# Low parts of k stored for both heads over all 128 partitions, in a block with stick-breaking attention

## The chip, the cores and the metric

The kernel runs on one core of a Trainium2 chip, as one launch. The metric is the device time in microseconds (us); the time before is the median of three runs. One further execution was taken with a profiler; all durations of single instructions come from it. The core has five engines that run their own instruction streams and wait for one another through semaphores: TensorE (PE in the profile, its weight loads PEld), VectorE (DVE), ScalarE (ACT), GpSimd (POOL) and SyncE (SP), which here only issues DMAs.

## The reference

A transformer block on 1024 positions of width 1024: attention over 8 heads of 64 beside a gated linear recurrence, then an MLP with squared ReLU. What the change concerns is the score product in the attention:

```python
def stick_breaking_attention(q, k, v):
    ...
    for blk in range(S // BLOCK_Q):
        q0 = blk * BLOCK_Q
        end = q0 + BLOCK_Q
        z = jnp.einsum('bqhd,bkhd->bhqk', qf[:, q0:end], kf[:, :end]) * scale
        ...
        mask = kpos < qpos
        log_one_minus = jnp.where(mask, jax.nn.log_sigmoid(-z), 0.0)
        suffix = lax.cumsum(log_one_minus, axis=3, reverse=True) - log_one_minus
        log_w = jax.nn.log_sigmoid(z) + suffix
        w = jnp.where(mask, jnp.exp(log_w), 0.0)
        outs.append(jnp.einsum('bhqk,bkhd->bqhd', w, vf[:, :end]))

def hybrid_mixer(h, w_in, ...):
    proj = h @ w_in
    q, k, v, xl, gl = jnp.split(proj, ...)
    q = rms_norm(q.reshape(B, S, N_ATTN_HEADS, HEAD_DIM), q_norm_g)
    k = rms_norm(k.reshape(B, S, N_ATTN_HEADS, HEAD_DIM), k_norm_g)
    ...
    attn = stick_breaking_attention(q, k, v).reshape(B, S, ATTN_WIDTH)
    xl = causal_depthwise_conv(xl, conv_w, conv_b)
    lru = rg_lru(xl, ...) * jax.nn.gelu(gl)
    return jnp.concatenate([attn, lru], axis=-1) @ w_out
```

## The kernel before

**Split operands.** Products that need more than one pass's precision are made of parts. A value is written as a high part in the format fp32r and a low part, the rest (`lo_part`, L59: a subtraction on an engine that is passed in). Most products add three matmuls (`mm3`, L70): low by high, high by low, high by high.

**Stages.** The input is normalised and transposed into `hTh` and `hTl` (high and low). For each of four pairs of heads `p`, `in_proj` (L193) projects 256 positions at a time (`tp` from 0 to 3) to q, k and v. The recurrence follows (`lru_tile`), then the attention of the four pairs mixed with the in-projection of the next pair and with the gates (`gate`, L479); then the out-projection (`po`) and the MLP in two groups (`up_group`, `down_group`). `ORDER` (L34) names the sequence in which the jobs of the attention stage are written: I is an in-projection, A an attention job (pair, head of the pair, block of 256 queries), G a gate, O and W loads of weights, Y a DMA that sums parts of the MLP's weights. The kernel is built by a scheduler, which sets the order on each engine from its own estimate of times; a changed instruction can therefore move others.

**In-projection.** After the norm, `qs` holds for each head its high part of q beside its low part, 64 columns each; `ks` holds the high part of k twice, and `kl` the low part of k once, for both heads of the pair side by side. Transposes on TensorE (matmuls with the identity `identr`) turn them into banks of PSUM: `pq`, `pk` with four each, `pl` with two. Copies bring the banks to `qT` and `kH` (2 x 256 columns) and `kL` (256 columns). All three banks are the one buffer of the pool `ps_t`, so they follow each other. In `qT[:, h]` 64 partitions hold the high part of q and the other 64 its low part; in `kH[:, h]` both halves hold the high part of k. In `kL`, 64 partitions belong to each head.

**Attention.** For a row block of 128 queries and up to 512 keys (`k0`), two matmuls make the scores `z`: L431 over all 128 partitions gives (high + low of q) by high of k, and L432 over the head's 64 partitions `hs` gives high of q by low of k. The block on the diagonal adds the mask by a third matmul (L434). Two sigmoids on ScalarE follow (L436, L437), a running product from the right on VectorE (L441) and a product on GpSimd (L442). The weights `w` are transposed (`pw`, L452), split (`wth`, `wtl`) and multiplied by v (`av`, L461); `ob` goes to the array `mix_d` in DRAM. There are 96 such score blocks.

**Gates.** `gate(c, ch)` loads two arrays (`gx` of `rs_d`, `hl` of `lru_d`), makes a projection `pgl` from `hTh` and `hTl`, and works on VectorE (L487, L489), ScalarE and GpSimd (L491, L492). Its tiles are buffers of the in-projection: `gx` has the tag `raw`, `hl` that of `ks` or `kl`. The loads of `x1` (L586), for the out-projection, go into the place of `hTh`, and so wait for the last gate's projection; on SP they stand in one queue with all other loads.

Of the kernel before, what the change touches and what calls it, by code (L numbers as in the profile page):

```python
# [10 lines left out]
F32R = mybir.dt.float32r  # L11
# [8 lines left out]
P = 128  # L20
S = 1024
D = 1024
NT = S // P
KC = D // P
HD = 64
# [18 lines left out]
def kernel(ctx, tc, x, norm1_g, w_in, conv_w, conv_b, w_rg, b_rg, w_ig, b_ig,  # L44
                             lam, q_norm_g, k_norm_g, w_out, norm2_g, w_up, w_down, out):
    nc = tc.nc
# [12 lines left out]
    def lo_part(eng, lo, src, hi):  # L59
        ins = eng.tensor_tensor(lo, src, hi.bitcast(F32), op=ALU.subtract)  # L60
        if eng is nc.gpsimd:
            mark(ins)
# [4 lines left out]
    def mark(ins):  # L67
        marked[:] = [ins.ins]
# [13 lines left out]
    ps_t = pool(ctx, "ps_t", bufs=1, space=PSUM)  # L82

    def bank(pl, shape, name):
        return pl.tile([P] + shape, F32, tag=pl.name, name=name)
# [33 lines left out]
    identr = const.tile([P, P], F32R, name="identr")  # L119
# [35 lines left out]
    mp = pool(left1, "misc")  # L155
# [32 lines left out]

    def in_proj_open(p, qp):
        return (qp.tile([P, 2, S], F32R, tag="qT", name=f"qT{p}"), qp.tile([P, 2, S], F32R, tag="kH", name=f"kH{p}"),  # L190
                qp.tile([P, S], F32R, tag="kL", name=f"kL{p}"), qp.tile([P, NT, 2, P], F32R, tag="vv", name=f"vv{p}"))

    def in_proj(p, qkv, ws, tp):  # L193
        qT, kH, kL, vv = qkv
        raw = mp.tile([P, 2, 4, HD], F32, tag="raw", name=f"raw{p}{tp}", bufs=2)
        for tt in range(2):
            t = 2 * tp + tt
            pd = bank(ps_d, [384], f"pd{p}{t}")
            for kc in range(KC):
                wh, wl = ws[kc]  # L200
                mm3(pd, hTh[:, kc, t * P:(t + 1) * P], hTl[:, kc, t * P:(t + 1) * P], wh, wl, kc == 0, kc == KC - 1)
            rs = rstd1[:, t:t + 1]
            nc.scalar.mul(raw[:, tt].rearrange("p a d -> p (a d)"), pd[:, 0:256], rs)
            pvv = pd[:, 256:384].rearrange("p (h d) -> p h d", h=2)
            nc.scalar.mul(vv[:, t, :, 0:HD], pvv, rs)
            nc.vector.scalar_tensor_tensor(vv[:, t, :, HD:P], pvv, rs, vv[:, t, :, 0:HD].bitcast(F32), op0=ALU.mult, op1=ALU.subtract)  # L206
        sq = mp.tile([P, 8, HD], F32, tag="sq", name=f"sq{p}{tp}")
        raw8 = raw.rearrange("p t a d -> p (t a) d")
        nc.vector.tensor_tensor(sq, raw8, raw8, op=ALU.mult)
        ssq = small.tile([P, 8], F32, tag="ssq8", name=f"ssq{p}{tp}")  # L210
        nc.vector.tensor_reduce(ssq, sq, axis=AX.X, op=ALU.add)
        rstd = rsqrt_mean(ssq, HD, 8)
        nc.vector.tensor_tensor(raw8, raw8, rstd.unsqueeze(2).broadcast_to([P, 8, HD]), op=ALU.mult)
        nc.gpsimd.tensor_tensor(raw[:, :, 0:2, :], raw[:, :, 0:2, :], qkg, op=ALU.mult)
        qs = mp.tile([P, 2, 2, 2, HD], F32R, tag="qs", name=f"qs{p}{tp}")
        ks = mp.tile([P, 4, 2, HD], F32R, tag="ks", name=f"ks{p}{tp}")
        kl = mp.tile([P, 2, 2, HD], F32R, tag="kl", name=f"kl{p}{tp}")
        for h in range(2):
            nc.scalar.copy(qs[:, :, h, h, :], raw[:, :, h, :])
            lo_part(nc.vector, qs[:, :, h, 1 - h, :], raw[:, :, h, :], qs[:, :, h, h, :])  # L220
        for tt in range(2):
            nc.scalar.copy(ks[:, 2 * tt:2 * tt + 2], raw[:, tt, 2:4, :].unsqueeze(2).broadcast_to([P, 2, 2, HD]))
            lo_part(nc.gpsimd, kl[:, tt], raw[:, tt, 2:4, :], ks[:, 2 * tt:2 * tt + 2, 0, :])
        cols = slice(256 * tp, 256 * tp + 256)
        pq = bank(ps_t, [2, 256], f"pq{p}{tp}")
        for h in range(2):
            for tt in range(2):
                nc.tensor.matmul(pq[:, h, tt * P:(tt + 1) * P], qs[:, tt, h].rearrange("p a d -> p (a d)"), identr, start=True, stop=True)
        nc.scalar.copy(qT[:, :, cols], pq)
        pk = bank(ps_t, [2, 256], f"pk{p}{tp}")  # L230
        for h in range(2):
            for tt in range(2):
                nc.tensor.matmul(pk[:, h, tt * P:(tt + 1) * P], ks[:, 2 * tt + h].rearrange("p a d -> p (a d)"), identr, start=True, stop=True)
        nc.vector.tensor_copy(kH[:, :, cols], pk)
        pl = bank(ps_t, [256], f"pl{p}{tp}")
        for tt in range(2):
            nc.tensor.matmul(pl[:, tt * P:(tt + 1) * P], kl[:, tt].rearrange("p a d -> p (a d)"), identr, start=True, stop=True)
        nc.vector.tensor_copy(kL[:, cols], pl)


    right1 = ExitStack()
# [97 lines left out]
    for tp in range(2, NT // 2):  # L339
# [4 lines left out]
        if tp == 3:  # L344
            scale_row(1)
        in_proj(0, qkv0, wpair, tp - 1)
    in_proj(0, qkv0, wpair, NT // 2 - 1)
    xstack.close()

# [64 lines left out]
    def attention(p, h, c, qkv):  # L414
        qT, kH, kL, vv = qkv
        hs = slice(HD * h, HD * h + HD)
        os = slice(HD - HD * h, P - HD * h)
        wrow = []
        for r in (2 * c, 2 * c + 1):
            n = (r + 1) * P  # L420
            wps = {}
            nxt = None
            qr = slice(r * P, (r + 1) * P)
            for k0 in range((n - 1) // 512 * 512, -1, -512):
                kn = min(n - k0, 512)
                diag = k0 + kn == n
                g = ap.tile([P, 516], F32, tag="g", name=f"g{p}{h}{r}{k0}", bufs=NG)
                w = ap.tile([P, 512], F32, tag="w", name=f"w{p}{h}{r}{k0}", bufs=NW)
                wps[k0 // 512] = w
                z = bank(ps_z, [512], f"z{p}{h}{r}{k0}")[:, :kn]  # L430
                nc.tensor.matmul(z, qT[:, h, qr], kH[:, h, k0:k0 + kn], start=True, stop=False)  # L431
                nc.tensor.matmul(z, qT[hs, h, qr], kL[hs, k0:k0 + kn], start=False, stop=not diag)  # L432
                if diag:
                    nc.tensor.matmul(z[:, kn - P:kn], identb, maskb, start=False, stop=True)  # L434
                    nc.gpsimd.memset(g[:, kn:kn + 1], 1.0)
                nc.scalar.activation(g[:, :kn], z, AF.Sigmoid, scale=-1.0)  # L436
                nc.scalar.activation(w[:, :kn], z, AF.Sigmoid)  # L437
                if not diag:
                    nc.vector.tensor_copy(g[:, kn:kn + 1], nxt)
                gr = g[:, :kn][:, ::-1]  # L440
                nc.vector.tensor_tensor_scan(gr, gr, gr, g[:, kn:kn + 1], op0=ALU.mult, op1=ALU.bypass)  # L441
                mark(nc.gpsimd.tensor_tensor(w[:, :kn], w[:, :kn], g[:, 1:kn + 1], op=ALU.mult))  # L442
                nxt = g[:, 0:1]
            wrow.append(wps)
        av = bank(ps_a, [256], f"av{p}{h}{c}")
        for m in range(c + 1):
# [11 lines left out]
            for jj in range(2):  # L458
                q0 = P if jj == 1 and m == c else 0
                for wt in (wtl, wth):  # L460
                    nc.tensor.matmul(av[:, q0:256], vv[:, 2 * m + jj, h, :], wt[:, 256 * jj:256 * jj + 256 - q0],  # L461
                                     start=m == 0 and jj == 0 and wt is wtl,
                                     stop=m == c and jj == 1 and wt is wth)
# [411 lines left out]
```

## Time and profile before

| what | time, us |
|---|---|
| median of the runs (1215.03 to 1216.63) | 1215.21 |
| the profiled execution | 1218.14 |
| its span, first to last instruction | 1216.4 |
| ahead of the first score product | 137 |
| score products, 96 blocks | 137 to 450 |
| from 540 to the end (rest of the out-projection, MLP) | 676 |

The profiled execution is 2.9 us above the median. In the profile a group's line gives source line, engine, operation and tiles (result <- operands), then the count, the busy time, the mean length of one and what the engine waited for ahead of it. "issue" is time in which an engine waited for nothing that the profile shows. A timeline gives the start and the length; matmuls overlap, so the time that one takes in a stream is read from start to start. 64*128 in a matmul's row means 64 rows of the array by 128 columns.

### The profile page before, as it was taken

How to read it: one execution, taken by the hardware profiler on the slowest of the kernel's cores; microseconds unless marked ns; L12 is line 12 of the kernel's file. 1: busy time of each engine (PE TensorE's matmuls, PEld its weight loads, DVE VectorE, ACT ScalarE, POOL GpSimd, SP SyncE). 2: the span in 40 equal slices, each digit the busy share in tenths (PEclk: the TensorE clock that was granted, in tenths of full speed). 3: DMA queues.
4: the chain of work that ended last, by engine and by line, in shares of the span. 5: the costliest groups of instructions: out<-in, count | busy, mean ns of one | idle time of the engine just before them, and what ended most of it. 6: DMA issues, size and time to landing. Idle time of an engine off the chain costs nothing.

```text
span 1216.4 us, 15273 instructions
## 1 busy us (share of the span) xinstructions
PE 1150.6 (95%) x5410; PEld 948.0 (78%) x5410; DVE 897.3 (74%) x1182; ACT 568.5 (47%) x991; POOL 586.5 (48%) x472
## 2 busy tenths in 40 slices
PE   7998899999999988998999989889999999999998
PEld 7976777789987766886888767678887887878887
DVE  6889997999898788226387769685843876699663
ACT  7554475665665564144433554233334335733331
POOL 1356764574355566102645746533317368483240
PEclk9999999799999978998999989989999999999999
DMA  8110026824505275200453788944412345442531
GB/s 262 48 49 35 18 96 130 227 66 145 122 5 112 89 256 181 101 1 35 141 188 130 201 241 287 224 142 139 141 35 87 122 144 191 158 148 73 193 132 69
DMA packets 91659, 157.05 MB, mean 129 GB/s; under 512 B 8848, under 2 KB 27328, under 8 KB 91584
## 3 DMA queue, kind: packets, MB, share of 16 engines
q1 hardware_dynamic: 79040, 122.54, 30.5%
q0 software_dynamic: 12544, 33.56, 11.8%
q8 instruction: 42, 0.69, 0.2%
q14 instruction: 33, 0.27, 0.1%
HBM read 145.58 MB, written 44.04 MB: 156 GB/s over the span
## 4 chain that ended last, share of the span: by engine, by line
PE 69%; DVE 13%; issue 8%; DMA 3%; POOL 3%; ACT 3%; SPq 0%; DVEq 0%; ACTq 0%; POOLq 0%
PE p L633 22%; PE pa L633 11%; PE pb L633 5%; PE pc L633 4%; PE pd L71 3%; PE pd L72 3%; PE pd L73 3%; PE po L71 3%; PE po L72 2%; PE po L73 2%; PE av L461 2%; PE z L432 2%; PE pw L452 2%; DVE g L441 2%; DVE sl_u L60 2%
## 5 line engine op out<-in xcount | busy, mean ns | idle before, releaser
L442 POOL TENSOR_TENSOR w<-w,g 128x128 f32<-128x128 f32 (+3 forms) x96 | 99.7, 1044 | 107.7 <-DVE g L441 52.7
L60 DVE TENSOR_TENSOR ml_p<-rp,mh_p 128x1024 fp32r<-128x1024 f32 x56 | 110.3, 1971 | 28.1 <-ACT mh_p L544 28.1
L441 DVE TENSOR_TENSOR_SCAN g<-g 128x128 f32<-128x128 f32 (+3 forms) x96 | 112.6, 1185 | 8.0 <-ACT g L436 5.4
L544 ACT CAST sh_p<-U 128x1024 fp32r<-128x1024 f32 x48 | 50.5, 1051 | 131.0 <-PE pa L633 59.2
L633 PE MATMUL pa<-mh_p,sl_p 128*128 128x512 f32 x256 | 100.7, 393 | 7.1 <-DVE sl_p L60 6.8
L767 POOL TENSOR_TENSOR rp<-rp,qp 128x1024 f32<-128x1024 f32 x24 | 69.0, 2876 | 70.3 <-DMA qp<-in_w_down_dram 39.8
L633 PE MATMUL pa<-ml_p,sh_p 128*128 128x512 f32 x256 | 100.3, 392 | 0.0
L633 PE MATMUL pa<-mh_p,sh_p 128*128 128x512 f32 x256 | 100.1, 391 | 0.0
L71 PE MATMUL pd<-wh_p,hTl 128*128 128x384 f32 x256 | 90.9, 356 | 7.3 <-DVE vv L206 5.0
L72 PE MATMUL pd<-wl_p,hTh 128*128 128x384 f32 x256 | 89.8, 351 | 0.1
L73 PE MATMUL pd<-wh_p,hTh 128*128 128x384 f32 x256 | 88.3, 345 | 0.0
L60 DVE TENSOR_TENSOR sl_p<-U,sh_p 128x1024 fp32r<-128x1024 f32 x38 | 63.4, 1668 | 30.7 <-ACT sh_p L544 30.7
L737 POOL TENSOR_TENSOR ru<-ru,rv 128x1024 f32<-128x1024 f32 x16 | 43.8, 2769 | 58.9 <-DMA rv<-sum_u 58.8
L544 ACT CAST mh_p<-rp 128x1024 fp32r<-128x1024 f32 x56 | 58.7, 1048 | 21.3 <-POOL rp L767 14.6
L633 PEld LDWEIGHTS pa<-mh_p,sl_p 128*128 128x128 f32 x256 | 48.5, 189 | 18.2 <-DVE sl_p L60 7.5
L662 POOL TENSOR_TENSOR U<-U 128x512 f32<-128x512 f32 x32 | 47.0, 1501 | 32.0 <-ACT U L660 32.0
L456 ACT CAST wth<-pw 128x512 fp32r<-128x512 f32 (+1 forms) x80 | 42.4, 545 | 38.0 <-PE pw L452 24.8
L436 ACT ACTIVATE g<-z 128x384 f32<-128x384 f32 (+3 forms) x96 | 47.8, 497 | 22.9 <-PE z L434 10.4
L71 PEld LDWEIGHTS pd<-wh_p,hTl 128*128 128x128 f32 x256 | 49.4, 193 | 11.0 <-DVE vv L206 6.7
L660 ACT ACTIVATE U<-U 128x512 f32<-128x512 f32 x48 | 30.0, 628 | 58.6 <-DVE U L721 31.1
L60 DVE TENSOR_TENSOR wtl<-pw,wth 128x512 fp32r<-128x512 f32 (+1 forms) x80 | 49.5, 629 | 9.5 <-ACT wth L456 8.9
L633 PEld LDWEIGHTS pa<-mh_p,sh_p 128*128 128x128 f32 x256 | 48.5, 189 | 10.2
(325 smaller groups left out, 3566.7 us busy)
## 6 DMA issues: line engine op xcount, KB each, us to landing
sum_u<-in_w_up_dram POOLq DMA_DIRECT2D x8, 2048.0 KB, 12.7
sum_d<-in_w_down_dram POOLq DMA_DIRECT2D x8, 2048.0 KB, 13.3
rp<-in_w_down_dram SPq DMA_DIRECT2D x32, 512.0 KB, 4.1
rp<-sum_d SPq DMA_DIRECT2D x24, 512.0 KB, 5.4
ra<-in_w_up_dram SPq DMA_DIRECT2D x16, 512.0 KB, 4.4
qp<-in_w_down_dram SPq DMA_DIRECT2D x16, 512.0 KB, 4.2
wr_p<-in_w_in_dram SPq DMA_DIRECT2D x24, 192.0 KB, 5.8
xt<-in_x_dram SPq DMA_DIRECT2D x8, 512.0 KB, 7.5
```

The costliest lines, as they stand in the source:

```text
L60: ins = eng.tensor_tensor(lo, src, hi.bitcast(F32), op=ALU.subtract)
L71: nc.tensor.matmul(ps, al, bh, start=start, stop=False)
L72: nc.tensor.matmul(ps, ah, bl, start=False, stop=False)
L73: nc.tensor.matmul(ps, ah, bh, start=False, stop=stop)
L436: nc.scalar.activation(g[:, :kn], z, AF.Sigmoid, scale=-1.0)
L441: nc.vector.tensor_tensor_scan(gr, gr, gr, g[:, kn:kn + 1], op0=ALU.mult, op1=ALU.bypass)
L442: mark(nc.gpsimd.tensor_tensor(w[:, :kn], w[:, :kn], g[:, 1:kn + 1], op=ALU.mult))
L544: nc.scalar.copy(hl[0], src)
L633: nc.tensor.matmul(ps, x_, y_, start=start and n == 0, stop=stop and n == 2, skip_group_check=True)
L662: mark(nc.gpsimd.tensor_tensor(c, c, c, op=ALU.mult))
L737: mark(nc.gpsimd.tensor_tensor(r, r, q, **add))
L767: mark(nc.gpsimd.tensor_tensor(r, r, q, **add))
```

## The change

The low part of k is stored like the high part: `kl` holds it twice per head, `pl` has four transposes in place of two, `kL` is [128, 2, 1024] instead of [128, 1024], and the second score product runs over all 128 partitions. It then also adds low of q by low of k, which the kernel left out before.

```diff
@@ in_proj_open
-                qp.tile([P, S], F32R, tag="kL", name=f"kL{p}"), qp.tile([P, NT, 2, P], F32R, tag="vv", name=f"vv{p}"))
+                qp.tile([P, 2, S], F32R, tag="kL", name=f"kL{p}"), qp.tile([P, NT, 2, P], F32R, tag="vv", name=f"vv{p}"))
@@ in_proj
-        kl = mp.tile([P, 2, 2, HD], F32R, tag="kl", name=f"kl{p}{tp}")
+        kl = mp.tile([P, 4, 2, HD], F32R, tag="kl", name=f"kl{p}{tp}")
...
-            lo_part(nc.gpsimd, kl[:, tt], raw[:, tt, 2:4, :], ks[:, 2 * tt:2 * tt + 2, 0, :])
+            lo_part(nc.gpsimd, kl[:, 2 * tt:2 * tt + 2], raw[:, tt, 2:4, :].unsqueeze(2).broadcast_to([P, 2, 2, HD]),
+                    ks[:, 2 * tt:2 * tt + 2])
...
-        pl = bank(ps_t, [256], f"pl{p}{tp}")
-        for tt in range(2):
-            nc.tensor.matmul(pl[:, tt * P:(tt + 1) * P], kl[:, tt].rearrange("p a d -> p (a d)"), identr, start=True, stop=True)
-        nc.vector.tensor_copy(kL[:, cols], pl)
+        pl = bank(ps_t, [2, 256], f"pl{p}{tp}")
+        for h in range(2):
+            for tt in range(2):
+                nc.tensor.matmul(pl[:, h, tt * P:(tt + 1) * P], kl[:, 2 * tt + h].rearrange("p a d -> p (a d)"), identr, start=True, stop=True)
+        nc.vector.tensor_copy(kL[:, :, cols], pl)
@@ attention
-                nc.tensor.matmul(z, qT[hs, h, qr], kL[hs, k0:k0 + kn], start=False, stop=not diag)
+                nc.tensor.matmul(z, qT[:, h, qr], kL[:, h, k0:k0 + kn], start=False, stop=not diag)
```

The scheduler moves rows as well. Lines of the changed kernel are up to 2 higher (L432 is L434, L487 is L489). The numbers after a tile's name are pair, head and blocks, then the tile's own.

TensorE in the first in-projection, before (`pd06` is a projection, `pl00` the bank of the low part of k):

```order
L72 MATMUL pd06_786<-wl_p0_6_206,hTh_100 128x384
L237 MATMUL pl00_411<-identr_84,kl00_390 128x128 x2
L73 MATMUL pd06_786<-wh_p0_6_205,hTh_100 128x384
L71 MATMUL pd06_786<-wh_p0_7_211,hTl_101 128x384
L72 MATMUL pd06_786<-wl_p0_7_212,hTh_100 128x384
```

and now:

```order
L72 MATMUL pd06_792<-wl_p0_6_206,hTh_100 128x384
L239 MATMUL pl00_411<-identr_84,kl00_390 128x128 x4
L73 MATMUL pd06_792<-wh_p0_6_205,hTh_100 128x384
L71 MATMUL pd06_792<-wh_p0_7_211,hTl_101 128x384
L72 MATMUL pd06_792<-wl_p0_7_212,hTh_100 128x384
```

The place is the same, with two transposes more. On SP, late in the attention, before (`gx`, `hl` are a gate's loads, `ob` results of attention, `x1` loads for the out-projection):

```order
L484 DMA hl20_5267<-lru_d_88 128x512
L483 DMA gx30_5340<-rs_d_89 128x512
L469 DMA mix_d_87<-ob301_4588 64x256
L484 DMA hl30_5341<-lru_d_88 128x512
L493 DMA mix_d_87<-hl20_5267 128x512
L484 DMA hl21_5304<-lru_d_88 128x512
L483 DMA gx31_5377<-rs_d_89 128x512
L493 DMA mix_d_87<-hl30_5341 128x512
L586 DMA x1_5423<-in_x_dram 128x512
L484 DMA hl31_5378<-lru_d_88 128x512
```

and now:

```order
L471 DMA mix_d_87<-ob301_4618 64x256
L486 DMA hl20_5299<-lru_d_88 128x512
L588 DMA x1_5455<-in_x_dram 128x512 x5
L485 DMA gx30_5372<-rs_d_89 128x512
L486 DMA hl30_5373<-lru_d_88 128x512
L588 DMA x1_5455<-in_x_dram 128x512
L495 DMA mix_d_87<-hl20_5299 128x512
L588 DMA x1_5455<-in_x_dram 128x512
```

Five loads of `x1` stand ahead of `gx30`, where none stood before. On VectorE at the same place, before (`gx`, `ge` are the gate's steps, `g` scans, `wtl` low parts of attention weights):

```order
L441 SCALAR_TENSOR_TENSOR g3040_4755<-g3040_4755 128x512
L487 TENSOR_TENSOR gx30_5340<-pgl30_5344,gx30_5340 128x512
L489 SCALAR_TENSOR_TENSOR ge21_5332<-ge21_5332,gx21_5303 128x512
L489 SCALAR_TENSOR_TENSOR ge30_5369<-ge30_5369,gx30_5340 128x512
L60 TENSOR_TENSOR wtl2132_4667<-pw2132_4661,wth2132_4666 128x512
L60 TENSOR_TENSOR wtl2133_4679<-pw2133_4674,wth2133_4678 128x384
L441 SCALAR_TENSOR_TENSOR g305512_4765<-g305512_4765 128x256
```

and now:

```order
L491 SCALAR_TENSOR_TENSOR ge21_5364<-ge21_5364,gx21_5335 128x512
L60 TENSOR_TENSOR wtl3110_4750<-pw3110_4744,wth3110_4749 128x512
L443 SCALAR_TENSOR_TENSOR g314512_4966<-g314512_4966 128x128
L469 TENSOR_TENSOR ob213_4717<-av213_4664,ot213_4716 64x256
L489 TENSOR_TENSOR gx30_5372<-pgl30_5376,gx30_5372 128x512
L60 TENSOR_TENSOR wtl3111_4762<-pw3111_4757,wth3111_4761 128x384
L441 COPY g3140_4977<-g314512_4966 128x1
```

The step `gx30` has moved from behind the scan of head 0, row block 4 of pair 3 to behind that of row block 5 and the first of head 1, and `ge30` behind it; `gx31` and `ge31` follow among the scans of the last row blocks. From the out-projection on, the order of all engines is as before.

## The prediction

> **What bounds the kernel now.** I read the page's busy shares first, then the busy time by stretch, then the chain that ended last inside those stretches, and last the timeline of TensorE where the changed instructions stand.
>
> ```profile
> PE 1150.6 (95%) x5410; PEld 948.0 (78%) x5410; DVE 897.3 (74%) x1182; ACT 568.5 (47%) x991; POOL 586.5 (48%) x472
> ...
> core 0: us, PE busy (x) PEld busy (x) DVE busy (x) ACT busy (x) POOL busy (x), PEclk, DMA share, GB/s
> 137.00:450.00 313.00, 295.72 (x1614) 243.11 (x1612) 278.90 (x506) 185.44 (x448) 177.24 (x241) 0.94 0.45 123
> ...
> 137.00:230.00 93.00, 83.80 (x446) 67.42 (x444) 85.62 (x154) 52.07 (x129) 51.66 (x74) 0.96 0.44 120
> 230.00:360.00 130.00, 130.00 (x744) 112.25 (x742) 117.47 (x230) 79.79 (x194) 68.69 (x96) 0.93 0.40 103
> 360.00:450.00 90.00, 81.92 (x427) 63.43 (x426) 75.81 (x124) 53.58 (x125) 56.89 (x72) 0.94 0.51 153
> ```
>
> The whole program is TensorE's, but the change touches only the stage with the score products, 137 to 450 us. There TensorE is idle for 313 - 295.7 = 17.3 us and VectorE for 313 - 278.9 = 34.1 us. So VectorE stands close behind: no saving on TensorE can be worth more than about 34 us, and much less if VectorE's idle time is waiting that stays. In the middle stretch (230 to 360) TensorE never rests; in the outer two it waits too.
>
> ```profile
> by line: PE pd L73 16.0%; PE pd L71 15.9%; PE pd L72 15.7%; PE av L461 13.5%; PE z L432 12.5%; PE pw L452 11.5%; PE z L431 7.6%; PE z L434 3.3%; PE pq L228 1.8%; PE pk L233 1.6%; PE pl L237 0.7%
> ...
> by line: issue 16.0%; DVE g L441 15.3%; PE av L461 5.2%; PE z L432 4.8%; DMA gx<-rs_d 4.6%; DVE wtl L60 4.0%; PE pgl L72 3.9%; DMA wr_gl<-in_w_in_dram 3.9%; PE pgl L71 3.7%; PE pgl L73 3.6%; PE z L431 3.4%; PE pw L452 2.9%; POOL w L442 2.9%
> ```
>
> The first of these is the chain of 230:360, all TensorE; the second is that of 360:450, where the chain goes through scans, products, loads and launch gaps in turn.
>
> **What the change removes.** TensorE's timeline (start, length), then the weight loads of the same moment:
>
> ```profile
> 212.27 0.28 PE L461 MATMUL av<-wth,vv 128*128 128x256 f32 x1
> 212.39 0.22 PE L461 MATMUL av<-wtl,vv 128*128 128x128 f32 x1
> ...
> 212.94 0.48 PE L431 MATMUL z<-kH,qT 128*128 128x512 f32 x1
> 213.35 0.50 PE L432 MATMUL z<-kL,qT 64*128 64x512 f32 x1
> 213.78 0.39 PE L431 MATMUL z<-kH,qT 128*128 128x256 f32 x1
> 214.10 0.38 PE L432 MATMUL z<-kL,qT 64*128 64x256 f32 x1
> 214.41 0.23 PE L434 MATMUL z<-maskb,identb 128*128 128x128 bf16 x1
> ...
> 214.76 0.39 PE L72 MATMUL pgl<-hTl,wh_gl 128*128 128x512 f32 x1
> 214.99 0.40 PE L73 MATMUL pgl<-hTh,wh_gl 128*128 128x512 f32 x1
> ```
>
> ```profile
> 213.35 0.18 PEld L432 LDWEIGHTS z<-kL,qT 64*128 64x128 f32 x1 [0.24 <-issue]
> 213.78 0.19 PEld L431 LDWEIGHTS z<-kH,qT 128*128 128x128 f32 x1 [0.24 <-issue]
> ...
> 214.76 0.19 PEld L73 LDWEIGHTS pgl<-hTh,wh_gl 128*128 128x128 f32 x1
> ...
> PEld z L432 <- issue: 17.1, 68, 0.4
> ```
>
> In the stream of L71 to L73 the weights of the matmul that starts at 214.99 are loaded from 214.76, under the matmul before: starts lie 0.23 us apart at 512 columns, 0.12 at 256 (212.27 to 212.39). Around a 64-row product this fails twice: its own load starts only with it (213.35), and the load of the next matmul waits until it is through (213.78). The pair L431, L432 takes 213.78 - 212.94 = 0.84 us at 512 columns against 0.46 for two whole-array products, and 214.41 - 213.78 = 0.63 at 256 against 0.24. The longer step ahead of 213.35 is in part the first load after the transposes, some 0.08, which stays. So a pair saves about **0.30 us**. Of the 96 pairs, 48 have 512 columns, 16 each 384, 256 and 128; for the last, where the loads themselves set the pace, I estimate 0.20 from the same rows. 80 x 0.30 + 16 x 0.20 makes **27.2 us** of TensorE time, between nothing (the third rival) and 48 x 0.38 + 32 x 0.39 + 16 x 0.20 = 34 if the longer first step went whole.
>
> The Trainium skill, TensorEngine Tiling (Array Packing), section Key Properties, says that a change of tiling mode drains TensorE; the two late loads above agree. Against it stands TensorE: Matmul & The Clock Gate, section Why this matters for your kernels: "K=32 single mm = same time as K=128". By that rule a 64-row product costs what a 128-row one does and the saving is nil; the rows at 213.35 and 213.78 speak against it, and its time is the third rival's.
>
> **What it adds.**
>
> ```profile
> L237 PE MATMUL pl<-identr,kl x32: 222/275/327, 47.9 to 411.9; 128*128 128x128 f32 x32
> L238 DVE CAST kL<-pl x16: 387/410/426, 48.3 to 413.3; 128x256 fp32r<-128x256 f32 x16
> ...
> L234 DVE CAST kH<-pk 128x512 fp32r<-128x512 f32 x16 | 10.8, 672 | 0.6 <-PE pk L233 0.6
> ...
> L60 POOL TENSOR_TENSOR kl<-raw,ks x32: 453/463/1789, 33.1 to 391.5; 128x128 fp32r<-128x128 f32 x32
> L214 POOL TENSOR_TENSOR raw<-raw,qkg x16: 728/740/751, 32.4 to 390.4; 128x256 f32<-128x256 f32 x16
> ...
> 211.70 0.56 PE L228 MATMUL pq<-identr,qs 128*128 128x128 f32 x4
> 212.10 0.34 PE L461 MATMUL av<-wtl,vv 128*128 128x256 f32 x1
> ```
>
> - TensorE: 32 more `pl` transposes of 128 columns. Four such (L228) take 212.10 - 211.70 = 0.40 us, so 32 x 0.10 = 3.2 us. Net saving on TensorE: 27.2 - 3.2 = **24 us**; 295.7 becomes 271.7.
> - VectorE: 16 copies of `kL` grow to the size of the `kH` copy: 16 x (0.672 - 0.410) = **4.2 us**.
> - GpSimd: 32 differences `kl` double. The nearest 256-element row is L214: 32 x (0.740 - 0.463) = 8.9 us. GpSimd has 313 - 177 = 136 us idle in the stage, which hides it; without that cover it would cost the 8.9. But a second price is possible:
>
> ```profile
> L60 DVE TENSOR_TENSOR wl_p<-wr_p,wh_p x16: 543/842/1733, 8.4 to 315.1; 128x384 fp32r<-128x384 f32 x16
> ```
>
> The same VectorE difference takes 0.54 us at best, 0.84 in the median and 1.73 at worst. How much VectorE loses to the 8.9 us of extra GpSimd work lies between 0 and 8.9; since its scans and PSUM copies hold more of this stage than such differences, I take 2.5. The Trainium skill, GPSIMD Engine Reference, section 1 Specifications, has GpSimd's SBUF interface shared with VectorE, with contention for VectorE instructions with two SBUF inputs; the spread of this row fits, though no run here has tied it to GpSimd.
>
> VectorE's need in the stage becomes 278.9 + 4.2 + 2.5 = **285.6 us**, above TensorE's 271.7. The bound changes hands.
>
> - The order: the gates of the last two channel tiles come later. On SP the load `gx30` now stands behind five loads of `x1`, on VectorE the gate's rows stand among the last scans.
>
> ```profile
> 434.93 6.05 SPq L586 DMA_DIRECT2D x<-in_x_dram  x8
> ...
> x<-in_x_dram SPq DMA_DIRECT2D x16, 256.0 KB, 4.8
> ...
> gx<-rs_d SPq DMA_DIRECT2D x8, 256.0 KB, 3.2
> ...
> DVE gx L487 <- DMA gx<-rs_d: 4.5, 3, 3.3
> ```
>
> Five issues at 6.05 / 8 = 0.76 us, then a landing of 3.2 to 4.8: `gx30` comes up to 8 us after the last gate product, which releases the `x1` loads. What is queued ahead of it on VectorE (two scans, two differences, a copy: some 5 us by like rows) covers most of that; an uncovered rest of 0 to 3 us holds up `wtl3111` and TensorE's `av` behind it. Before, such waits were 4.5 us in all. On the other side, moving the gate's rows out of the crowded part may gain as much. I take +0.5, bounds -3 and +3.
>
> **The sum.** Two ways. (a) By the whole stage: the engine that bounds it had 17.3 of 313 us idle, 5.5%. If VectorE at 285.6 us does as well, the stage takes 285.6 / 0.945 = 302.2, a gain of 10.8. (b) By stretches: in 230:360 VectorE needs 117.5 plus 5 of 16 copies (1.3) plus 1, 119.8; at 94.5% that is 126.8, gain 3.2. In 360:450 L432 and L431 hold 8.2% of the chain, 7.4 us, of which 0.30 / 0.84 go: gain 2.6. In 137:230 VectorE is the busier engine already: about 0.5. Together 6.3. Ahead of 137 the first four copies cost up to 1. Between (a) and (b), with the order's +0.5, I take **-7.7 us**. The profiled execution took 1218.1 us (span 1216.4 and 1.7 around it), so 1210.4; the median of the runs shown is 1215.2, 2.9 below that execution, and the forecast for it is **1207.5**.
>
> **The rivals.**
> - *TensorE's saving arrives whole.* For it: TensorE has no idle time in 230:360. Against: VectorE would have to be busy 285.6 of 313 - 24 = 289 us, 99%, which no stretch above shows. 1215.2 - 24 + 1 = 1192.
> - *VectorE takes it all.* Its 34 us of idle are chain latencies (scan to GpSimd to transposes) and stay. Then the faster products only wait longer. Gain within 2.4 of nothing: 1215.
> - *The 64 rows cost nothing* and the change doesn't speed up TensorE: then 3.2 us of transposes are added where TensorE never rests or a copy behind them; with part hidden, 1218.
> - *Slower: VectorE's queue is the path.* Each longer `kL` copy and each stretched difference delays all that is queued behind it, scans above all: 4.2 + 2.5 = +6.7, 1222. It decides if VectorE's idle time does not shrink when TensorE gets faster; with the toll at its bound of 8.9 it would be +13.
>
> **Chances.** Forecast (-3 to -16) 0.60; saving whole 0.08; nothing within 0.2% (2.4 us, about what a measurement of this kernel can tell from no change) 0.14; 64 rows free 0.05; slower 0.13. That is faster 0.68, same 0.14, slower 0.18. The range runs from 1196, short of the whole saving, to 1220, which takes in the smaller half of the slower case; about 2 in 10 stay outside. The forecast's own range is 1199 to 1212.
>
> **What would show it.** In the changed profile the weights of the second score product (L432, in the changed file L434) should load ahead of their matmuls, the "issue" wait of that group fall from 17.1 us to near nothing, and a pair of 512 columns take about 0.54 us. VectorE should be the busier engine of the stage, at 93 to 96%. The `kL` copies should read near 0.67 us, GpSimd's `kl` near 0.74. After the stage (450 us on) lengths should be as before. I am wrong if the pair still takes 0.84, if VectorE's share of the stage stays at 89%, or if a wait for `gx` of more than 3 us stands among the last scans.

## The result, and the profile after

The changed kernel takes **1229.8 us** in the median of four runs (1226.5 to 1234.2), against 1215.1 for the kernel before beside it: a ratio of 1.0122, 95% interval 1.0088 to 1.0156. It is slower by some 15 us, where 1207.5 had been forecast. The profiled execution took 1234.2 us.

The busy shares and the chain of the changed kernel's page, and its attention stage by stretch (columns as in the prediction; the stage now runs from 148 to 460):

```profile
PE 1134.5 (92%) x5442; PEld 953.0 (77%) x5442; DVE 911.6 (74%) x1182; ACT 565.0 (46%) x991; POOL 598.8 (49%) x472
...
PE 57%; DVE 19%; issue 9%; DMA 7%; POOL 5%; ACT 3%; SPq 0%; DVEq 0%; POOLq 0%; ACTq 0%
...
148.00:460.00 312.00, 275.10 (x1636) 244.19 (x1634) 279.58 (x497) 180.97 (x446) 183.43 (x235) 0.94 0.44 117
```

TensorE is busy 16 us less than before, and the program is longer all the same. The stage is as long as it was (312 us against 313), with 20 us less TensorE work in it. VectorE is now the busier engine, at 279.6 of 312 us, 89.6%: the same share as before, 89.1%.

The pair of score products in the changed kernel's timeline, matmuls and then weight loads:

```profile
188.12 0.48 PE L433 MATMUL z<-kH,qT 128*128 128x512 f32 x1
188.44 0.40 PE L434 MATMUL z<-kL,qT 128*128 128x512 f32 x1
188.68 0.23 PE L436 MATMUL z<-maskb,identb 128*128 128x128 bf16 x1
...
188.21 0.19 PEld L434 LDWEIGHTS z<-kL,qT 128*128 128x128 f32 x1
```

The weights of L434 are loaded at 188.21, ahead of their matmul at 188.44 and under the first product. A pair of 512 columns takes 188.68 - 188.12 = 0.56 us, where it took 0.84. So TensorE does what the change is for. The loss lies elsewhere, and the lag begins ahead of the attention. The first score product, by its line in the trace of before and then of the changed kernel (first and last start behind the durations):

```profile
L431 PE MATMUL z<-kH,qT x96: 221/440/775, 137.2 to 445.5; 128*128 128x512 f32 x48, 128*128 128x128 f32 x16, 128*128 128x256 f32 x16, 128*128 128x384 f32 x16
```

```profile
L433 PE MATMUL z<-kH,qT x96: 221/422/776, 148.2 to 455.7; 128*128 128x512 f32 x48, 128*128 128x128 f32 x16, 128*128 128x256 f32 x16, 128*128 128x384 f32 x16
```

Attention starts 11.0 us late, before a single one of the changed products has run. The lag is still 10.2 us when the last score product starts, and 16.0 at the end (spans 1232.4 and 1216.4): the attention stage makes up hardly any of it, and some 6 us more come behind the last score product.

### The profile page after: what moved, and what is told of

It reads as the page before. It is cut to its first block, busy times and chain, and to the rows that moved or that the text cites. A ratio compares the mean times of both kernels' runs of the same rounds, so it can differ in the third digit from the quotient of the medians.

```text
span 1232.4 us, 15333 instructions
## 1 busy us (share of the span) xinstructions
PE 1134.5 (92%) x5442; PEld 953.0 (77%) x5442; DVE 911.6 (74%) x1182; ACT 565.0 (46%) x991; POOL 598.8 (49%) x472
## 4 chain that ended last, share of the span: by engine, by line
PE 57%; DVE 19%; issue 9%; DMA 7%; POOL 5%; ACT 3%; SPq 0%; DVEq 0%; POOLq 0%; ACTq 0%
PE p L635 19%; PE pa L635 10%; PE pb L635 5%; PE pc L635 4%; DVE g L443 3%; PE po L71 2%; PE po L72 2%; PE po L73 2%; DMA gx<-rs_d 2%; PE pd L71 2%; PE pd L73 2%; PE pd L72 2%; DVE sl_u L60 1%; DVE sl_p L60 1%; PE av L463 1%
## 5 line engine op out<-in xcount | busy, mean ns | idle before, releaser
L444 POOL TENSOR_TENSOR w<-w,g 128x128 f32<-128x128 f32 (+3 forms) x96 | 105.3, 1104 | 93.7 <-DVE g L443 65.2
L443 DVE TENSOR_TENSOR_SCAN g<-g 128x128 f32<-128x128 f32 (+3 forms) x96 | 115.2, 1211 | 3.7 <-ACT g L438 1.1
L73 PE MATMUL pd<-wh_p,hTh 128*128 128x384 f32 x256 | 91.0, 355 | 0.0
L454 PE MATMUL pw<-ident,w 128*128 128x128 f32 x288 | 48.4, 288 | 9.1 <-DVE wtl L60 8.6
L463 PE MATMUL av<-wtl,vv 128*128 128x256 f32 (+1 forms) x160 | 46.5, 314 | 11.0 <-DVE wtl L60 6.4
```

The source lines that it names most:

```text
L73: nc.tensor.matmul(ps, ah, bh, start=False, stop=stop)
L454: nc.tensor.transpose(pw[:, i * P:(i + 1) * P], wrow[rr][j // 4][:, j % 4 * P:(j % 4 + 1) * P], ident)
```

## The experiments

Times are medians; a ratio is to runs of the kernel before on the same chip. The kernel before took 1215.2 to 1216.9 us on the chips used, so gains and losses in us are worked out from ratios (times 1215.2) unless spans or two medians are named. Kernels that "follow an order" carry a table of ranks for each engine, from which every instruction of an engine gets the one ahead of it as a predecessor in the schedule. This adds no instruction, and no time that shows: the kernel before with such a table of its own order, and one load moved, takes 1216.2 us (1.0004, below).

```diff
+        for x, y in zip(row, row[1:]):
+            tc.add_manual_dep(y, x.name, mybir.DependencyInfo(mybir.DependencyClass.NoSync, ...), reason="order")
```

### Parts of the change, and its order as a whole

The second product over 64 rows again, all else as changed:

```diff
-                nc.tensor.matmul(z, qT[:, h, qr], kL[:, h, k0:k0 + kn], start=False, stop=not diag)
+                nc.tensor.matmul(z, qT[hs, h, qr], kL[hs, h, k0:k0 + kn], start=False, stop=not diag)
```

> The changed kernel, with the second score product over 64 rows again (it reads one half of the doubled low parts); all added work and the changed order of all engines stay. Theory A (the loss comes from the order that the scheduler gave the changed program): 1230 us plus what the whole-array product had saved in it, so 1230 to 1245. Theory B (the loss comes from the added work on VectorE and GpSimd): the same, since that work stays. What it tells is the saving of the whole-array product under the changed order: 0 if VectorE takes all of it, up to 24 us if TensorE bounds the stage.

Only the second product changed in the kernel before (`kL` as it was; all engines keep their order):

```diff
-                nc.tensor.matmul(z, qT[hs, h, qr], kL[hs, k0:k0 + kn], start=False, stop=not diag)
+                nc.tensor.matmul(z, qT[:, h, qr], kL[:, k0:k0 + kn], start=False, stop=not diag)
```

> The kernel before, with one edit: the second score product runs over all 128 partitions of the old, undoubled kL. It so adds low of q by the low of k of the pair's other head, a term of the order of a low part squared, which the kernel before leaves out. No work is added and the order of all engines is that of before. Both theories: faster than before. By the sum of the prediction the saving of TensorE is 27 us and half-hidden by VectorE: 1200 to 1210. If VectorE's idle time does not shrink, 1213 to 1217. If 64 rows cost no more than 128, 1215.

The changed code in the order of before (a pair of added transposes stands behind the pair that was there), and the code of before in the changed order:

> The changed kernel with all its instructions, in the order of the kernel before on every engine (edges of issue order alone; the 32 added transposes stand behind the two of their bank). Theory A (order): the loss of 14.7 us goes and the saving shows, 1203 to 1213. Theory B (added work): still slower than before, 1222 to 1232.

> The kernel before with its own instructions, in the order of the changed kernel on every engine (edges of issue order alone). Theory A (order): slower than before by about the loss and the saving together, 1230 to 1245. Theory B (added work): as before within 4 us, 1211 to 1219.

| kernel | median, us | ratio, 95% interval |
|---|---|---|
| changed, 64 rows | 1231.1 | 1.0115 (1.0089 to 1.0141) |
| whole-array product alone | 1209.5 | 0.9942 (0.9919 to 0.9965) |
| changed code, order of before | 1218.1 | 1.0011 (0.9993 to 1.0030) |
| code of before, changed order | 1230.5 | 1.0099 (1.0063 to 1.0135) |

The product alone gains 7.0 us (0.58%) and beats both kernels. With the added work, in the order of before, that gain is used up; 1218.1 lies between the ranges of theories A and B, so each has a part of the cause. The order alone, without any of the change's work, loses 12.0 us (0.99%), as theory A had it. In that order the product is worth nothing: with 64 rows and with 128 the times are within each other's intervals, although TensorE's busy time differs by 25 us between them (here the page of the 64-row kernel, against 1134.5 of the changed one):

```profile
PE 1159.4 (94%) x5442; PEld 953.2 (77%) x5442; DVE 907.4 (74%) x1182; ACT 568.2 (46%) x991; POOL 601.7 (49%) x472
```

### The added work, split

GpSimd's doubling without the rest, in before's order, on top of the whole-array product:

```diff
-        kl = mp.tile([P, 2, 2, HD], F32R, tag="kl", ...)
+        kl = mp.tile([P, 2, 2, 2, HD], F32R, tag="kl", ...)
-            lo_part(nc.gpsimd, kl[:, tt], raw[:, tt, 2:4, :], ...)
+            lo_part(nc.gpsimd, kl[:, tt].rearrange("p d a e -> p a d e"), raw[:, tt, 2:4, :].unsqueeze(2).broadcast_to([P, 2, 2, HD]), ...)
```

> The kernel that changes only the second score product (1209.5 us, in before's order), with one thing more: GpSimd writes kl twice (32 subtractions over 128x2x2x64 instead of 128x128), and only the first copy is transposed. Low parts of q meet low parts of the other head's k in the product, as in that kernel, so the sums differ in their smallest terms. With all of the added work in before's order the time was 1218.1, 8.6 us more. Theory G (it is GpSimd's longer subtractions, through what waits for kl or through the port that it shares with VectorE): 1215 to 1219. Theory V (it is VectorE's copies of kL, 16 x 0.26 us, and TensorE's 32 transposes, 3.2 us): 1209 to 1211.

And the converse, `kl` as before, but transposed twice into a bank of 512 columns:

```diff
+                nc.tensor.matmul(pl[:, h, tt * P:(tt + 1) * P], kl[:, tt].rearrange("p a d -> p (a d)"), identr, start=True, stop=True)
+        nc.vector.tensor_copy(kL[:, :, cols], pl)
```

> The converse: GpSimd writes kl once as before, TensorE transposes it twice (32 transposes more) and VectorE copies 512 instead of 256 columns into kL, which is as large as in the change; in before's order, with the second score product over 128 partitions (both copies are the same here, so low parts of q meet low parts of the other head's k in it). Theory G: 1209 to 1212. Theory V: 1215 to 1219. If the two split the 8.6 us by their busy time (GpSimd 8.9 us, VectorE 4.2 and TensorE 3.2 us added), about 1213.

GpSimd's doubling: 1219.0 us, ratio 1.0030 (1.0014 to 1.0047). The copies and transposes: 1213.7, 0.9986 (0.9969 to 1.0003). Against the product alone that is +10.7 and +5.3 us, each good to some 3.5. The first stands at the top of theory G's range, the second near the 1213 that was foretold if both share the cost. Together they cost 8.4, so they do not add; why is open. What GpSimd's part does to VectorE can be read in three traces: first the product alone, its page and two groups of VectorE in the attention stage (count, busy time, mean ns), then the same with GpSimd's doubling, then with all of the added work in before's order:

```profile
PE 1122.5 (93%) x5410; PEld 943.5 (78%) x5410; DVE 896.5 (74%) x1182; ACT 566.3 (47%) x991; POOL 582.2 (48%) x472
...
L441 DVE TENSOR_TENSOR_SCAN g<-g 128x512 f32<-128x512 f32 x48 | 69.6, 1452 | 2.5 <-POOL g L435 0.7 <-ACT g L436 0.4
L60 DVE TENSOR_TENSOR qs<-raw,qs 128x128 fp32r<-128x128 f32 x24 | 9.6, 435 | 1.7 <-ACT qs L219 1.7
```

```profile
PE 1123.5 (92%) x5410; PEld 942.7 (77%) x5410; DVE 903.7 (74%) x1182; ACT 565.4 (46%) x991; POOL 597.0 (49%) x472
...
L442 DVE TENSOR_TENSOR_SCAN g<-g 128x512 f32<-128x512 f32 x48 | 71.2, 1485 | 2.2 <-POOL g L436 0.7 <-ACT g L437 0.2
L60 DVE TENSOR_TENSOR qs<-raw,qs 128x128 fp32r<-128x128 f32 x24 | 10.8, 483 | 1.7 <-ACT qs L219 1.7
```

```profile
PE 1126.1 (93%) x5442; PEld 947.3 (78%) x5442; DVE 901.9 (74%) x1182; ACT 566.0 (47%) x991; POOL 597.4 (49%) x472
...
L445 DVE TENSOR_TENSOR_SCAN g<-g 128x512 f32<-128x512 f32 x48 | 69.4, 1450 | 2.0 <-ACT g L440 0.8
L60 DVE TENSOR_TENSOR qs<-raw,qs 128x128 fp32r<-128x128 f32 x24 | 10.8, 483 | 1.7 <-ACT qs L219 1.7
```

VectorE's differences of `qs` stretch from 435 to 483 ns in both kernels that double GpSimd's work, 1.2 us in all. The rest does not repeat. With the doubling alone VectorE runs the same 1182 instructions and is busy 7.2 us longer (903.7 against 896.5), its scans at 1485 ns. With the same doubling in the third trace the scans are at 1450, as without it, and of the 5.4 us more the longer copies make 4.2; some 1.2 are left. So the toll that the prediction bounded by 0 and 8.9 came out at 1.2 and at 7.2 in one execution each, and its size is not settled. Nor is it shown by what way the doubling takes 10.7 us of time.

### Where the order costs: early or late

Now the code of before, with the changed order on every engine either from the first score product on, or up to it:

> The code of before; on every engine the order of before up to the first score product of attention, and the order of after from there on. All of before's code in the order of after took 1230.5 us against before's 1216.9, so the order alone costs some 13 us; its trace lagged before's by 6.7 us when the first score product started and by 9 at three fifths of the attention. Theory A (the loss arises in the recurrence stage, where the reciprocals, the convolution rows and the gate products of the recurrence stand in another order): this kernel keeps that stage as it was and takes 1215 to 1220. Theory B (the loss arises in attention, where the gates of the second half are projected later and gx30 stands behind five other transfers, the term that the prediction priced at -3 to +3): 1226 to 1231. If both stages share it: 1220 to 1226.

> The code of before; the converse: the order of after up to the first score product, the order of before from there on. Theory A: 1225 to 1231, with the first score product some 7 us later than in before, as in the full order of after. Theory B: 1215 to 1220. If both stages share it, this and the kernel with the late part add up to 13 us over before.

Both lose: 1226.5 us, 1.0091 (1.0059 to 1.0122) for the late part, 1225.7, 1.0088 (1.0058 to 1.0117) for the early one. Neither theory foresaw two losses that each come near the whole. Taken apart further, engine by engine:

> The code of before in its own order, but TensorE alone follows the order of after up to the first score product. With all engines in that early order the time was 1225.7 (10.5 us over before), and in its trace TensorE waited 5.4 us at pg20r and 4.0 us at pg30r for VectorE's convolution rows. Theory P (it is TensorE's queue: the gate products now stand ahead of the input projection of the next head pair, and hold it up): 1221 to 1226. Theory D (it is VectorE's queue: reciprocals of 3.3 us now stand ahead of the convolution rows, and TensorE only shows the delay): 1214 to 1218.

> The converse: VectorE alone follows the order of after up to the first score product, the other engines that of before. Theory P: 1214 to 1218. Theory D: 1221 to 1226. If it takes both (reciprocals ahead on VectorE and gate products ahead on TensorE), this and the kernel with TensorE alone both stay within 3 us of before.

> The code of before in its own order, but TensorE alone follows the order of after from the first score product on (the gates of the second half of the tokens projected later, score products moved around them). With all engines in that late order the time was 1226.5, 11.2 us over before. If TensorE's order is what costs there: 1222 to 1228. If it is what the other queues do (the loads of the next pair's weights, which ScalarE awaited for 10.1 us in that trace): 1214 to 1218.

TensorE's early order alone: 1222.2, 1.0047 (1.0029 to 1.0065). VectorE's: 1230.4, 1.0108 (1.0079 to 1.0136), no less than all engines' together; TensorE waits 8.5 us at `pg30r` in it. So each engine's early order costs by itself, and neither theory P nor D has it right. TensorE's late order alone costs 60 us (1278.0; 1.0495, 1.0458 to 1.0531). That says nothing of the change: an order made to fit the other engines' is waited out when these keep theirs. The two early orders taken alone are to be read with the same caution.

Then the repair that should have worked, the changed code with before's early order:

> The changed code, with the order of before on every engine up to the first score product and its own order from there on. Theory A (the recurrence stage holds most of the loss, as the lag of 10.8 us at the first score product in its trace has it): 1219 to 1223. Theory O (the losses of the two stages overlap, as the two half orders say, which cost 11.2 and 10.5 us each and 13 together): 1226 to 1230, since attention in the later order then loses its own 11.

1230.7 us, 1.0106 (1.0073 to 1.0139): nothing came back, as theory O had it, although the first score product starts at 137.8 us, as early as in before. Something in attention takes the 10 us if the recurrence does not.

### The late part: one load

The trace of the code of before with the late order (1226.5 us) has it. Timeline of SyncE, GpSimd and ScalarE (start, length, and in brackets the idle time ahead), then TensorE's wait:

```profile
222.80 4.10 SPq L163 DMA_DIRECT2D wr_p<-in_w_in_dram  x4
...
223.46 1.30 POOL L147 DMA_DIRECT2D sum_u<-in_w_up_dram  x1 [0.26 <-issue]
...
237.51 0.51 ACT L164 CAST wh_p<-wr_p 128x384 fp32r<-128x384 f32 x1 [10.13 <-DMA wr_p<-in_w_in_dram]
...
PE z L431 <- ACT w L437: 8.0, 1, 8.0
```

`wr_p` are four loads of 192 KB, weights of the next head pair. GpSimd starts a 2 MB load of `w_up` between the first and the last of them, and ScalarE stands 10.1 us before the copy of the last. The one of them that has its landing in the trace took 13.0 us from issue to landing. Behind it wait the sigmoids, and TensorE 8.0 us for a bank of scores. In the kernel before, the same four are out before that load starts:

```profile
219.54 2.47 SPq L163 DMA_DIRECT2D wr_p<-in_w_in_dram  x4
...
225.41 1.30 POOL L147 DMA_DIRECT2D sum_u<-in_w_up_dram  x1
```

The Trainium skill, DMA: Bandwidth & Descriptors, section Issuing engines are not separate DMA queues, says that transfers begun by different engines run on the same 16 DMA engines and interleave; the 10.1 us agree. To test it, that one load was moved on GpSimd, in the order's table alone, seven instructions down (four up in the kernel before):

> The kernel with the code of before and the order of after from the first score product on (1226.5 us), with one row moved: the fourth 2 MB load of w_up on GpSimd's queue (sum_u, issued at 223.5 us in that trace, 0.7 us after the four loads wr_p of the next pair's weights began to be issued on SP) goes seven instructions later, behind the next gate product of the scores. Theory C (the loss of the later order is this collision: wr_p lands late, ScalarE stands 10.1 us before its copy wh_p, VectorE 6.5 and TensorE 8.0 us behind it): 1217 to 1221, and none of these waits is over 3 us. Theory S (the loss is spread over attention, VectorE being the bound): 1224 to 1228.

> The changed code with before's order up to the first score product and its own from there on (1230.7 us), with the same row moved. Theory C: 1221 to 1225, since its trace shows the same stop (TensorE 6.5 us at a score product behind ScalarE). Theory S: 1227 to 1231.

> The kernel before in its own order, with the same load moved the other way: four instructions earlier on GpSimd, which puts it from 225.4 to about 220 us, among the four loads of the next pair's weights (219.5 to 222 us). Theory C: ScalarE then stands several us before wh_p and the time goes to 1219 to 1225. Theory S: 1214 to 1218.

> The changed kernel in its own order throughout, with the same load moved seven instructions later. In its trace attention starts some 10 us later, ScalarE waits only 1.0 us for wr_p there, and no stop of TensorE follows. Both theories: 1227 to 1232; if it falls below 1225, the collision costs the changed kernel too, in runs that the one trace does not show.

| kernel | median, us | ratio, 95% interval |
|---|---|---|
| code of before, late order, load later | 1220.3 | 1.0041 (1.0025 to 1.0057) |
| changed, early order of before, load later | 1222.2 | 1.0066 (1.0041 to 1.0092) |
| before, load earlier | 1216.2 | 1.0004 (0.9981 to 1.0027) |
| changed, load later | 1230.4 | 1.0117 (1.0085 to 1.0149) |

The first came down by 6.1 us with one instruction moved, clear of the noise. The second came down by 8.5 us between medians but by 4.9 between ratios, each of which is good to 3 or 4, so its time alone does not settle it. In both traces the stop is gone: ScalarE waits at most 1.0 us for a `wr_p`, which takes 2.9 and 2.8 us to land, and TensorE's wait for a bank of scores (8.0 and 6.5 us) is not there. The control, the changed kernel with the load later, did not move. The third is no test: the load came at 222.45 us, behind all four `wr_p`, since it waits for the load ahead of it, so no collision was made. In the changed kernel the load starts just as the last of the four is issued, ScalarE waits for them only 1.0 us in all, and the collision is missed by a hair:

```profile
234.23 2.13 SPq L163 DMA_DIRECT2D wr_p<-in_w_in_dram  x4
...
236.10 1.30 POOL L147 DMA_DIRECT2D sum_u<-in_w_up_dram  x1 [1.47 <-DMA hl<-lru_d]
```

### The early part: two reciprocals

VectorE late in the recurrence, before and in the changed kernel (`u` are the rows of the convolution, six for a pass, that TensorE's gate products `pg30r` and `pg30i` need; the reciprocals belong to the pass before):

```profile
117.71 0.54 DVE L60 TENSOR_TENSOR wl_p<-rawB,wh_p 128x384 fp32r<-128x384 f32 x1
118.17 5.08 DVE L374 SCALAR_TENSOR_TENSOR u<-ext,vec,u 128x512 f32<-128x512 f32 x6
123.77 3.35 DVE L384 RECIPROCAL ext<-ext 128x512 f32<-128x512 f32 x1 [0.52 <-POOL ext L382]
```

```profile
124.67 3.34 DVE L386 RECIPROCAL ext<-ext 128x512 f32<-128x512 f32 x1
127.94 4.08 DVE L376 SCALAR_TENSOR_TENSOR u<-ext,vec,u 128x512 f32<-128x512 f32 x4
131.94 3.34 DVE L386 RECIPROCAL ext<-ext 128x512 f32<-128x512 f32 x1
135.20 2.32 DVE L376 SCALAR_TENSOR_TENSOR u<-ext,vec,u 128x512 f32<-128x512 f32 x2
```

The last row of `u` ends at 123.25 us before and at 137.52 now. Two reciprocals of 3.34 us stand ahead of it that stood behind. TensorE's waits for `u` in the changed kernel:

```profile
PE pg20r L379 <- DVE u L376: 5.1, 1, 5.1
...
PE pg30r L379 <- DVE u L376: 3.2, 1, 3.2
```

The first belongs to the pass before `pg30r`, and no reciprocal of the two stands ahead of its `u`. In the last two runs these two alone were moved, in the kernel before to where the changed order has them, and in the changed kernel back. VectorE's rows in the first of them:

```diff
 L60 TENSOR_TENSOR wl_p_7_1709<-rawB,wh_p_7_1708 128x384
+L384 RECIPROCAL ext_1194<-ext_1194 128x512
 L374 SCALAR_TENSOR_TENSOR u_1347<-ext_1291,vec,u_1347 128x512
 L374 SCALAR_TENSOR_TENSOR u_1347<-ext_1319,vec,u_1347 128x512
 L374 SCALAR_TENSOR_TENSOR u_1347<-ext_1291,vec,u_1347 128x512
 L374 SCALAR_TENSOR_TENSOR u_1347<-ext_1319,vec,u_1347 128x512
+L384 RECIPROCAL ext_1222<-ext_1222 128x512
 L374 SCALAR_TENSOR_TENSOR u_1347<-ext_1291,vec,u_1347 128x512
 L374 SCALAR_TENSOR_TENSOR u_1347<-ext_1319,vec,u_1347 128x512
-L384 RECIPROCAL ext_1194<-ext_1194 128x512
 L206 SCALAR_TENSOR_TENSOR vv_1716<-pd_1997,rstd_90,vv_1716 128x2x64
-L384 RECIPROCAL ext_1222<-ext_1222 128x512
```

> The kernel before in its own order, with two instructions moved on VectorE alone: the two reciprocals of the third pass of the recurrence (ext20 and ext21, 3.3 us each) stand where the order of after has them, the first ahead of the six convolution rows u3 and the second ahead of the last two of them, where before had both behind all six. VectorE's early order alone cost 13.8 us, and its trace has TensorE wait 8.5 us at pg30r for u3. Theory R (these two reciprocals are what costs): 1221 to 1228, with a wait of 6 us or more at pg30r. Theory M (the many smaller moves on VectorE add up): 1214 to 1219.

> The changed kernel in its own order, with the same two reciprocals put back behind the convolution rows u3. Theory R: the wait at pg30r (3.2 us in its trace) goes and the time is 1222 to 1227. Theory M: 1228 to 1232. If attention now starts early enough for the load of w_up to meet the weights of the next pair, the gain is given back there: 1227 to 1231 with a stop of ScalarE before wh_p.

Two instructions moved in the kernel before: 1229.0 us, 1.0101 (1.0078 to 1.0123), 12.3 us lost and a little more than theory R had. That is as much as the whole changed order costs on this code. VectorE and the score product in that kernel, and TensorE's wait:

```profile
123.76 3.35 DVE L384 RECIPROCAL ext<-ext 128x512 f32<-128x512 f32 x1 [5.00 <-POOL ext L382]
127.03 4.80 DVE L374 SCALAR_TENSOR_TENSOR u<-ext,vec,u 128x512 f32<-128x512 f32 x4
131.75 3.34 DVE L384 RECIPROCAL ext<-ext 128x512 f32<-128x512 f32 x1
135.01 2.32 DVE L374 SCALAR_TENSOR_TENSOR u<-ext,vec,u 128x512 f32<-128x512 f32 x2
...
L431 PE MATMUL z<-kH,qT x96: 221/444/776, 149.0 to 456.5; 128*128 128x512 f32 x48, 128*128 128x128 f32 x16, 128*128 128x256 f32 x16, 128*128 128x384 f32 x16
...
PE pg30r L377 <- DVE u L374: 7.8, 1, 7.8
```

VectorE stands idle for 5.0 us first, since the reciprocal's operand comes from GpSimd, with ready work behind it. Then the two reciprocals push `u` back, and TensorE waits 7.8 us at `pg30r` with the projections of the next pair queued behind. The first score product comes 11.8 us late, and the kernel ends 12.6 us late (span 1229.0 against 1216.4).

Put back in the changed kernel, the time is 1233.3, 1.0129 (1.0103 to 1.0155): no gain, and 2 us above the highest that was foretold. Its trace shows the stop of the third outcome that was written down for it:

```profile
231.68 4.08 SPq L163 DMA_DIRECT2D wr_p<-in_w_in_dram  x4
...
232.35 1.30 POOL L147 DMA_DIRECT2D sum_u<-in_w_up_dram  x1 [0.26 <-issue]
...
PE z L435 <- ACT w L441: 8.9, 1, 8.9
```

Attention starts 6.1 us earlier (142.1 against 148.2), and so the load of `w_up` falls between the loads of weights again; TensorE waits 8.9 us. The wait at `pg30r` is gone. That of 5.1 us at `pg20r` stays, and attention still starts 4.9 us later than in before, so the two reciprocals are not the whole of the early lag there. The changed kernel with both moves, the reciprocals back and the load later, was not run; what the reciprocals cost in it is thus shown as 6.1 us of lag and not as time.

## Why the prediction was wrong, step by step

- **TensorE's saving: right, and right in size.** 0.56 us for a pair against 0.54 foretold, the weights of L434 load ahead, and between 64 and 128 rows TensorE's busy time differs by 24.9 us in the changed order and by 28.1 in before's (1150.6 and 1122.5; 27.2 foretold). The sentence "K=32 single mm = same time as K=128" (the Trainium skill, TensorE: Matmul & The Clock Gate, section Why this matters for your kernels), which the prediction read for 64 rows, does not hold for a 64-row product among 128-row ones here: its pair takes 0.84 us against 0.56, and the whole-array product alone makes the kernel faster by 0.58%.
- **What the saving is worth: too much.** Sum (a) put VectorE at 94.5% of the stage once it bounds. It stayed at 89.6%, which the prediction had named as a sign that it is wrong. The product alone, in before's order, tests this best. From the first to the last score product VectorE is busy 272.6 of 302.2 us in its trace, 90.2%, against 275.3 of 308.7, 89.2%, in before's. By way (a) without the added work, 278.9 / 0.945 = 295.1, it would have gained 17.9 us; it gained 7.0. Way (b), by stretches, does better: 130 - 117.5 / 0.945 = 5.7, with the 2.6 and 0.5 of the outer stretches 8.8. VectorE's idle time is mostly waiting that stays, as the second rival said, but not all of it.
- **The added work: instructions right, toll not settled.** The copies read 674 ns and `kl` 740 ns in the median, as foretold. The toll on VectorE was taken at 2.5 us of bounds 0 to 8.9; it measured 7.2 us in one execution and 1.2 in another. The Trainium skill, GPSIMD Engine Reference, section 1 Specifications, has the two engines share their interface to SBUF, with contention for VectorE instructions with two SBUF inputs. The differences of `qs`, at 435 ns without the doubling and at 483 in both kernels with it, agree; the scans don't. All of the added work costs 8.4 us in before's order, where 6.7 of VectorE's time had been foretold, and cancels the gain: 1218.1 there, between the forecast and the slower rival's 1222. That rival had the direction right, but not the cause: with all of the change's work in before's order the kernel does not get to 1222.
- **The order: the step that failed.** It was taken at +0.5, bounds -3 and +3, from the two places that looked moved, the late gates and `gx30` among the last scans. VectorE waits for no load of `gx` there in the changed trace. The order costs 13.5 us on the changed code (1.0122 against 1.0011) and 12.0 on the code of before, far outside these bounds. The prediction priced the end of attention and looked at no row of the recurrence, where VectorE's queue had been reordered too, far from any changed line.

The parts, in ratios to before; each ratio is 0.2 to 0.35% uncertain, so a step is good to some 3 to 5 us:

| step | from | to | us |
|---|---|---|---|
| whole-array product | 1.0000 | 0.9942 | -7.0 |
| added work, order of before | 0.9942 | 1.0011 | +8.4 |
| late order, without the collision | 1.0011 | 1.0066 | +6.7 |
| early order | 1.0066 | 1.0122 | +6.8 |

What the 6.7 us of the late order are made of no run takes apart; on the code of before they are 5.0. The waits that differ most are two of TensorE's in the attention stage: for `wtl` ahead of `pw`, 8.7 us there against 3.2 in the order of before, and for `gx`, 9.3 against 4.2. A part lies at the end of attention, the place that the prediction did price. From the last score product to the first product of the out-projection the changed code takes 22.7 us with the late order (447.7 to 470.4, the load moved) and 16.9 in the order of before (445.1 to 462.0). In the other traces with the late order on all engines it is 18.6 to 22.8, in the others with before's 15.1 to 20.1. The changed kernel's VectorE has two steps of the gate among its last scans:

```profile
457.98 1.86 DVE L443 TENSOR_TENSOR_SCAN g<-g 128x512 f32<-128x512 f32 x1 [0.69 <-POOL g L437]
459.76 0.66 DVE L489 TENSOR_TENSOR gx<-pgl,gx 128x512 f32<-128x512 f32 x1
...
461.00 2.03 DVE L443 TENSOR_TENSOR_SCAN g<-g 128x512 f32<-128x512 f32 x1
...
464.13 1.39 DVE L491 SCALAR_TENSOR_TENSOR ge<-ge,gx 128x512 f32<-128x512 f32 x1
```

None of this was tried alone, nor why the product is worth nothing in the changed order. And the last row depends on the load: without its move, putting the early order right gains nothing (1.0106). With the load later in both kernels the early order costs 6.2 us (1.0117 against 1.0066).

## What to carry to other kernels

Where a scheduler sets the order, compare the order of the busy engines over the whole program, not only near the changed lines, and price every long instruction that has moved ahead of rows another engine waits for. Ask of each move whether its operand will be there: an instruction that waits at the head of a queue costs its wait and its length. And a gain upstream shifts everything behind it against the transfers that run on their own queue, so a repair that gains nothing may be right and have met the next collision; hold that one fixed before dropping the first.

## What was not expected of the hardware

- A 192 KB load that overlaps a 2 MB one from another engine's queue landed so late that its reader waited 10.1 us; such a load took 13.0 us to land, and 2.9 with the big one issued later, and that kernel was 6 us faster.
- With GpSimd's subtractions `kl` twice as long, VectorE's differences of `qs` (128x128) took 483 ns instead of 435 in both kernels of before's order that do so; its scans of 512 elements did not change in a way that repeats (1485 and 1450 ns, 1452 without).
- VectorE's reciprocal of 128x512 takes 3.34 us, where a convolution row of that size takes some 0.85 (six in 5.08).
